# First modulation in quarters beside three open column blocks; a quarter's weights split ahead of it; state space inputs and position tables loaded later

## The chip, the core and the metric

One NeuronCore of a Trainium2 chip runs the whole program. Its engines have a queue of instructions each: PE (matrix products; PEld is its weight load), DVE (vector), ACT (scalar), POOL, and SP, which here only issues DMAs. An instruction that waits holds up everything behind it in its own queue. The metric is the device time of one execution, in microseconds (us).

## The reference, cut to what matters

Two transformer blocks of width 2048 run over 256 tokens, all in f32. The front of the first one computes

```
sh1, sc1, g1, sh2, sc2, g2 = split(silu(c) @ w_ada + b_ada)   # c: one vector of 2048; w_ada: 2048 x 12288
h = rms_norm(x, norm_mix_g) * (1 + sc1) + sh1                 # 256 x 2048
u, q, k, v, ga, gb = split(h @ w_in)                          # w_in: 2048 x 8192; u, q, k, v: 1024 columns each
y = gelu(scan over tokens of a state space model of u)        # 64 groups of 16 channels, 64 complex states each
y_ssm = y * sigmoid(y @ w_glu + b_glu)                        # w_glu: 1024 x 1024
y_att = attention(q, k, v, rel_bias)                          # 8 heads
x = x + g1 * ((sigmoid(ga) * (y_ssm @ w_proj_ssm) + sigmoid(gb) * (y_att @ w_proj_attn)) @ w_out)
```

and then a feed forward part. The second block follows it, and ends in a sparse expert layer that gathers rows of two tables by index. Of the six modulation vectors only sc1 and sh1 (16 MB of w_ada each) are needed before h.

## The kernel before, in words

**Products.** A product of f32 precision is made of three of reduced precision. `piece` loads 1 MB of weights `w` (512 rows of k, 512 columns, as [128, 4, 512]) on the SP queue; ACT makes the high part `wh`, DVE the low part `wl` = w - wh. The activations are split likewise (`h1h`, `h1l` for the first block). For each of the four k-chunks and four column tiles of a piece PE runs three matmuls of 256 columns (the tokens): wh with h1h, wh with h1l, wl with h1h, 48 in all. `gemm` runs four pieces for 512 output columns of a product with k = 2048; two PSUM banks `ga` hold a block's sums. The pools of tiles have 4 buffers for `w` (tag W, shared by the modulation tiles `aw`), 2 for `wh` (H), 2 for `wl` (L), and 14 larger buffers of 1 MB (`unit`).

**The front.** `ada_pe` makes a modulation vector: 16 tiles `aw` of 128 rows by 2048 columns (1 MB each) come in, each goes through PE in four matmuls with f32 operands into `adap` (four column ranges of 512 on four groups of partitions, the same value in each row of a group), ACT copies `adap` to `adae`, four transposes bring it to columns (`adat`), and DVE adds the bias and, for sc1, 1 and the norm's gain, into `mod`. sc1 and sh1 run one after the other (lines 843 and 857). Beside them, paced by `bg`, run the input transposes (`x_in`), the parameters, tables (`ssm_table`, `tab`) and block operands (`ssm_blocks`, `bd` and `cd`, from `ssrc`) of the state space branch, and the position bias (`moba_bias`, `moba_flip`). When sc1 is there, `mod_scale` makes x * rstd * sc1 of a chunk (128 features) in place in `xT`; when sh1 is there, `mod_shift` makes `h1h` (ACT) and `h1l` (DVE) of each chunk:

```
    for i, _ in enumerate(ada_pe(1, 0, None, crep, pacc_, True)):
        if i < NC:
            mod_scale(xp, rstd, mods[(1, 1)], i, xp[i // 2][:, i % 2, :])
        bg(2.3, 0)
```

**What sets the order.** While `pinned[0]` is set, PE, DVE and ACT keep the written order of the instructions issued so far; a scheduler places those issued later, and may move them up between the pinned ones. SP's DMAs stand in one queue in the scheduler's order; each waits for the buffer it fills. After the front, `bg` is called between the matmuls of every piece and issues background work (state space rounds `ssm`, attention, later modulation vectors) by credits: `dve` us of vector work and `rate` modulation tiles a piece.

**After the front.** The blocks of u, q, k and v follow, then ga and gb. `ssm` makes, for four pairs of chunks, `bu` on PE, rotations with the tables on DVE, a scan, and `yp` on PE, which DVE adds into `uT`. Its gelu is split into `zhh` and `zhl`, the operand of the product with w_glu (line 986).

Of the kernel before, what the change touches and what calls it, by code (L numbers as in the profile page):

```python
# [31 lines left out]
def _consts():  # L32
    """Tables that depend on the shapes alone."""
# [40 lines left out]
# Pacing: vector engine time (us) of background work and modulation tiles for each piece of weights.  # L74
# [5 lines left out]
def tile_kernel(ctx: ExitStack, tc: tile.TileContext, I, out):  # L80
# [3 lines left out]
    class Pinned:  # L84
        """An engine whose instructions keep their traced order while `pinned` is set."""
# [52 lines left out]
    # ---------------------------------------------------------------- constants  # L138
# [33 lines left out]
    # ---------------------------------------------------------------- background work  # L172
    # Generators that yield the vector engine time (us) of what they have just issued.
# [39 lines left out]
    # ---------------------------------------------------------------- modulation vectors  # L213
# [31 lines left out]
    def ada(blk, j, g=None):  # L245
        """One modulation vector, its products on the vector engine."""
# [17 lines left out]
    def ada_pe(blk, j, g, crep, pool=pmisc, deep=False):  # L264
        """One modulation vector, its products on the tensor engine."""
# [11 lines left out]

    packs = [
# [24 lines left out]
    # state space parameters, the first modulation vector, the relative position table  # L303
    for t in range(2):
        SY.dma_start(xtok[t], I["x"][0, t * P:(t + 1) * P, :])
# [6 lines left out]
    g_sc1 = ada_pe(1, 1, "norm_mix_g", crep, pacc_, True)  # L312
    src = unit([P, 4, 512], "ssrc")

    def load_src():
        for k, n in enumerate(("ssm_b_re", "ssm_b_im")):
            SY.dma_start(src[:, k, :].rearrange("p (t q) -> p t q", t=32),
                        I[n][0].rearrange("(t g) n q -> (g n) t q", g=2))
        for k, n in enumerate(("ssm_c_re", "ssm_c_im")):
            SY.dma_start(src[:, 2 + k, :].rearrange("p (c n) -> p c n", c=8),  # L320
                        I[n][0].rearrange("(c g) q n -> (g q) c n", c=8))
# [10 lines left out]
    # ---------------------------------------------------------------- norm pieces  # L332
    def rsqrt_of(ps, scale, w, r1=None):
        """(scale ps (r1^2) + eps) ** -0.5 of w columns."""
# [16 lines left out]
    def spread(cols, dst):  # L351
        """Columns of one value a token to rows over the tokens, the same on all partitions."""
# [10 lines left out]
    class Rms:  # L363
        """Mean square over the features of feature-major pairs, a value a token."""
# [26 lines left out]
    def residual(xs, gcol, c, b, quick=False):  # L391
        """x chunks c, c+1 += gate * product."""
# [11 lines left out]
    class HL:  # L404
# [18 lines left out]
        def put2(self, c, src):  # L423
            """Chunks c and c+1 of the operand from an f32 pair."""
# [23 lines left out]
    # ---------------------------------------------------------------- matrix products  # L448
# [75 lines left out]
    # ------------------------------------------------ state space branch  # L524
    def exp_acc(x, shape, alloc):
        """(2^k, q) with exp(x) = 2^k (1 + q), by range reduction and a polynomial."""
# [18 lines left out]
    def ssm_prep():  # L545
# [66 lines left out]
        yield from ssm_table(0)  # L612
        for pp in range(2):
            bc = unit([P, 2, 2, 512], "bct")
            for k in range(2):
                cp2 = 2 * pp + k
                bct[cp2] = [bc[:, k, i, :].rearrange("p (r c m) -> p r c m", r=2, c=2) for i in range(2)]
                yield from ssm_blocks(cp2, src)
        for cp2 in range(1, 3):
            yield from ssm_table(cp2)  # L620

    def ssm_table(cp2):
        """cos and sin of 0..127 times each state's angle, for one pair of chunks (8 state tiles)."""
# [29 lines left out]
    def ssm_blocks(cp2, src):  # L653
        """Block diagonal operands of one pair of chunks."""
# [122 lines left out]
    bias = unit([P, 8, L], "bias")  # L777
# [29 lines left out]
    def x_in():  # L807
# [17 lines left out]
        yield 0.1  # L825

    g_x = start(x_in())
    g_ssm = start(ssm_prep())
    g_col = None
    for i, _ in enumerate(g_sc1):  # L830
        if i == 3:
# [873 lines left out]
```

## Time and profile before

| what | value |
|---|---|
| time, median of 3 runs | 3382.89 us (3382.7 to 3384.3) |
| the profiled execution's span, first to last instruction | 3379.9 us |
| granted TensorE clock, mean over it (1.0 is full speed) | 0.937 |
| busy, of the span: PE, DVE, ACT, POOL | 88%, 68%, 30%, 24% |
| chain that ended last: PE, DMA, issue, DVE, POOL | 62%, 23%, 6%, 4%, 4% |
| DMA traffic | 1068 MB, mean 316 GB/s |

The profiled execution's own time is not listed; its span lies 3.0 us under the median of the runs, and that is taken as what stands around the span. The page's busy shares are means over a front that is fed by transfers, a long middle in which PE is nearly always busy, and an end that gathers expert rows.

### The profile page before, as it was taken

What the parts mean: (1) busy time and instruction counts of PE and PEld (TensorE: products, weight loads), DVE (VectorE), ACT (ScalarE), POOL (GpSimd) and SP (SyncE); (2) the same over time, 40 slices, a digit from 0 to 9 for tenths busy, and PEclk for the clock granted to TensorE, in tenths of its full rate; (3) what the DMA queues carried; (4) which work ended last, traced back from release to release, by engine and by line L of the source; (5) the groups of instructions that cost most, each with busy time, mean ns of one, the idle gap of its engine ahead of it and who ended that gap; (6) DMA issues with size and microseconds to landing.
All of it is one profiled execution on the core that took longest, in us unless ns stands there. A gap on an engine that the chain in (4) does not pass through costs nothing.

```text
span 3379.9 us, 44134 instructions
## 1 busy us (share of the span) xinstructions
PE 2968.7 (88%) x18020; PEld 2299.5 (68%) x18020; DVE 2300.7 (68%) x3359; ACT 1024.1 (30%) x1360; POOL 794.3 (24%) x540
## 2 busy tenths in 40 slices
PE   6899999999999999999999999677876777667777
PEld 2687889999999999999999999333333333223233
DVE  7687779876778778865777668655655566664635
ACT  2323433444444444444347553111111101101100
POOL 1000000000000000000000003666665666665654
PEclk8899999999999999999999999898898889888888
DMA  9866667876899999864783447999999999999998
GB/s 368 301 220 214 202 234 248 305 266 217 295 328 337 320 322 325 324 238 166 259 276 102 138 150 291 418 421 422 421 421 422 422 421 422 421 421 409 422 374 355
DMA packets 278288, 1068.18 MB, mean 316 GB/s; under 512 B 27364, under 2 KB 31879, under 8 KB 187461
## 3 DMA queue, kind: packets, MB, share of 16 engines
q1 hardware_dynamic: 200258, 524.35, 44.3%
q0 software_dynamic: 74752, 538.26, 38.6%
q10 hardware_dynamic: 3076, 2.76, 0.3%
q8 instruction: 141, 2.31, 0.3%
q14 instruction: 61, 0.50, 0.0%
HBM read 1063.19 MB, written 2.11 MB: 315 GB/s over the span
## 4 chain that ended last, share of the span: by engine, by line
PE 62%; DMA 23%; issue 6%; DVE 4%; POOL 4%; ACT 1%; SPq 0%; POOLq 0%; DVEq 0%; ACTq 0%
PE ga L94 47%; DMA dn<-in_peer_down_dram,eid 12%; DMA up<-in_peer_up_dram,eid 9%; PE pe L94 6%; POOL dn L1599 2%; PE gb L94 2%; DMA aw<-in_w_ada_dram 2%; POOL up L1599 2%; PE adap L94 1%; DVE dn L94 1%; PE bu L94 1%; PE rms L94 1%; PE yp L94 1%; PE o L94 1%; PE cmp L94 0%
## 5 line engine op out<-in xcount | busy, mean ns | idle before, releaser
L94 PE MATMUL pe<-up,cdg 128*128 128x512 f32 x1936 | 914.4, 633 | 333.3 <-DMA up<-in_peer_up_dram,eid 202.3
L94 PEld LDWEIGHTS pe<-up,cdg 128*128 128x128 f32 x1936 | 387.7, 204 | 851.7 <-issue 636.7
L1599 POOL DMA_INDIRECT dn<-in_peer_down_dram,eid x256 | 397.7, 1554 | 2252.7 <-DVE rest L94 2003.0
L94 DVE TENSOR_TENSOR wl<-w,wh 128x2048 fp32r<-128x2048 f32 (+1 forms) x300 | 680.5, 2269 | 325.4 <-ACT wh L94 268.5
L94 ACT ACTIVATE wh<-w 128x2048 fp32r<-128x2048 f32 (+1 forms) x300 | 569.2, 1897 | 887.0 <-PE ga L94 715.4
L94 DVE SCALAR_TENSOR_TENSOR dn<-dn,htok 128x2048 f32<-128x2048 f32 x256 | 583.1, 2289 | 325.3 <-DMA dn<-in_peer_down_dram,eid 325.2
L1599 POOL DMA_INDIRECT up<-in_peer_up_dram,eid x256 | 383.6, 1499 | 276.1 <-PE pe L94 108.3
L94 DVE SCALAR_TENSOR_TENSOR acc<-aw,cT,acc 128x2048 f32<-128x2048 f32 x105 | 246.5, 2348 | 16.2 <-DMA aw<-in_ada_w_dram 10.2
L94 PE MATMUL ga<-h2h,wh 128*128 128x256 f32 x1024 | 250.1, 285 | 3.7 <-ACT h2h L94 3.7
L94 PE MATMUL ga<-h2l,wh 128*128 128x256 f32 x1024 | 249.6, 284 | 0.2 <-DVE h2l L94 0.2
L94 PE MATMUL ga<-ah,wh 128*128 128x256 f32 x1024 | 249.3, 283 | 0.0
L94 PE MATMUL ga<-al,wh 128*128 128x256 f32 x1024 | 249.0, 283 | 0.0
L94 ACT ACTIVATE cdg<-ca,cf 128x128 f32<-128x128 f32 x242 | 85.0, 394 | 488.9 <-PE pe L94 464.9
L94 PE MATMUL ga<-h1h,wh 128*128 128x256 f32 x896 | 224.0, 289 | 0.0
L94 PE MATMUL ga<-h1l,wh 128*128 128x256 f32 x896 | 220.4, 284 | 0.0
L94 PEld LDWEIGHTS ga<-h2h,wh 128*128 128x128 f32 x1024 | 197.3, 193 | 5.7 <-ACT h2h L94 4.0
L94 PEld LDWEIGHTS ga<-h2l,wh 128*128 128x128 f32 x1024 | 197.2, 193 | 0.5 <-DVE h2l L94 0.5
L94 PEld LDWEIGHTS ga<-ah,wh 128*128 128x128 f32 x1024 | 196.5, 192 | 0.8 <-ACT wh L94 0.8
L94 PEld LDWEIGHTS ga<-al,wh 128*128 128x128 f32 x1024 | 196.5, 192 | 0.0
L94 PEld LDWEIGHTS ga<-h1h,wh 128*128 128x128 f32 x896 | 172.7, 193 | 19.5 <-issue 15.3
L94 PEld LDWEIGHTS ga<-h1l,wh 128*128 128x128 f32 x896 | 172.9, 193 | 0.9 <-issue 0.8
L94 PE MATMUL ga<-h3h,wh 128*128 128x256 f32 x528 | 133.5, 291 | 1.1 <-ACT h3h L94 1.1
(443 smaller groups left out, 4581.4 us busy)
## 6 DMA issues: line engine op xcount, KB each, us to landing
w<-in_w_ff_dram SPq DMA_DIRECT2D x128, 1024.0 KB, 5.8
w<-in_w_in_dram SPq DMA_DIRECT2D x100, 1024.0 KB, 5.3
aw<-in_w_ada_dram SPq DMA_DIRECT2D x96, 1024.0 KB, 6.9
aw<-in_ada_w_dram SPq DMA_DIRECT2D x96, 1024.0 KB, 5.9
w<-in_w_out_dram SPq DMA_DIRECT2D x32, 1024.0 KB, 5.1
w<-in_peer_wq_dram SPq DMA_DIRECT2D x16, 1024.0 KB, 5.2
w<-in_w_proj_attn_dram SPq DMA_DIRECT2D x8, 1024.0 KB, 5.1
w<-in_w_proj_ssm_dram SPq DMA_DIRECT2D x8, 1024.0 KB, 6.2
```

The costliest lines, as they stand in the source:

```text
L94: r = f(*a, **k)
L1599: G.indirect_dma_start(out=rows_, out_offset=None, in_=table, in_offset=bass.IndirectOffsetOnAxis(ap=idx, axis=0))
```

## The change

`ada_quarter` replaces `ada_pe` for sc1 and sh1: a vector is made in four quarters of 512 columns, each of four tiles `aw` of 512 rows by 512 columns ([128, 4, 512], 1 MB, in pieces of 2 KB a row where they had 8 KB); two of three such tiles take a `unit` buffer, the third a W buffer. A quarter of `mod` gives four chunks of h. With them `first_part` runs one piece (four k-chunks) of three column blocks, u's two and q's first, whose sums stay open in six PSUM banks over all four quarters. The next quarter's tiles are issued between the matmuls of the first two blocks, and the weights of its first two pieces are loaded and split (`first_split`) before that quarter's chunks. x is loaded after two tiles; state space tables 0 and 1 are made beside the front; the loads of `ssrc`, the block operands with table 2, and the position table `moba_bias` are started after the front's code, `moba_flip` after the fourth block, and `ssm` after 16 pieces where it was 8.

```diff
+    def ada_quarter(blk, j, gi, dest, g):
+
+        ps = pmisc([P, 512], "adap")
+        sl = slice(4 * gi, 4 * gi + 4)
+        for k0 in range(0, NC, 4):
+            at[0] += 1
+            wt = wp.tile([P, 4, 512], F32, name=nm("aw"), tag="W") if at[0] % 3 == 0 else unit([P, 4, 512], "aw")
+            SY.dma_start(wt, adaw[blk][k0 * P:(k0 + 4) * P, j * D + 512 * gi:j * D + 512 * gi + 512]
+                         .rearrange("(c p) n -> p c n", p=P))
+            for q in range(4):
+                T.matmul(ps[32 * q:32 * q + 32, :], crep[:, k0 + q, :], wt[:, q, :],
+                         start=(k0 == 0), stop=(k0 == NC - 4), skip_group_check=True)
+            yield 0.0
+        ev = scr([P, 512], "adae")
+        S.copy(ev, ps)
+        pt = pmisc([P, 4, P], "adat")
+        for b in range(4):
+            T.transpose(pt[:, b, :], ev[:, 128 * b:128 * b + 128], ident)
+        V.tensor_reduce(dest[:, sl], pt.rearrange("p b (q r) -> p b q r", q=4)[:, :, :, 0], axis=AX.X, op=OP.add)
+        V.tensor_add(dest[:, sl], dest[:, sl], adab[blk][:, j * 16 + 4 * gi:j * 16 + 4 * gi + 4])
+        if g is not None:
+            V.scalar_tensor_tensor(dest[:, sl], dest[:, sl], 1.0, col[g][:, sl], op0=OP.add, op1=OP.mult)
+        yield 0.4
+
+    at = [0]
...
-    # state space parameters, the first modulation vector, the relative position table
-    for t in range(2):
-        SY.dma_start(xtok[t], I["x"][0, t * P:(t + 1) * P, :])
+    mods[(1, 1)], mods[(1, 0)] = (const([P, 16], "mod") for _ in range(2))
+    def first_mods(gi):
+        yield from ada_quarter(1, 1, gi, mods[(1, 1)], "norm_mix_g")
+        yield from ada_quarter(1, 0, gi, mods[(1, 0)], None)
+    def load_x():
+        for t in range(2):
+            SY.dma_start(xtok[t], I["x"][0, t * P:(t + 1) * P, :])
     ws = unit([P, 16, P], "ws")
     are, aim = ws[:32, 0, :], ws[:32, 1, :]
     S.dma_start(are, I["ssm_a_re"][0].rearrange("(t g) n -> t (g n)", g=2))
     S.dma_start(aim, I["ssm_a_im"][0].rearrange("(t g) n -> t (g n)", g=2))
     ld = tiny([32, 2], "ld")
     S.dma_start(ld, I["ssm_log_dt"][0].rearrange("(t g) -> t g", g=2))
-    g_sc1 = ada_pe(1, 1, "norm_mix_g", crep, pacc_, True)
-    src = unit([P, 4, 512], "ssrc")
+    src = []
     def load_src():
+        src.append(unit([P, 4, 512], "ssrc"))
...
-        yield from ssm_table(0)
+        for cp2 in range(2):
+            yield from ssm_table(cp2)
+
+    def ssm_operands():
         for pp in range(2):
             bc = unit([P, 2, 2, 512], "bct")
             for k in range(2):
                 cp2 = 2 * pp + k
                 bct[cp2] = [bc[:, k, i, :].rearrange("p (r c m) -> p r c m", r=2, c=2) for i in range(2)]
-                yield from ssm_blocks(cp2, src)
-        for cp2 in range(1, 3):
-            yield from ssm_table(cp2)
+                yield from ssm_blocks(cp2, src[0])
+        yield from ssm_table(2)
...
+        revs.append(unit([P, 8, L], "bias"))
...
-    g_x = start(x_in())
-    g_ssm = start(ssm_prep())
-    g_col = None
-    for i, _ in enumerate(g_sc1):
-        if i == 3:
-            load_src()
-        if i == 9:
-            g_col = start(columns())
-        if i == 6:
-            start(moba_bias())
-        if i == NC - 4:
-            drain(g_x, g_col)
-        bg(2.5, 0)
+    g_x = None
+    h = HL(16, "h1")
+    w_in = I["w_in"][0]
+
+    nfirst = 3
+    fb_ = [[(pacc_ if 2 * n + i < 3 else pmisc)([P, 2, L], "ga") for i in range(2)] for n in range(nfirst)]
+
+    def first_split(gi, n):
+        return piece(w_in, 4 * gi, 4, 512 * n, 512)
+
+    def first_part(gi, n, wp_, hook):
+        whi, wlo = wp_
+        for low in (False, True):
+            for i, b in enumerate(fb_[n]):
+                for kk in range(4):
+                    c = 4 * gi + kk
+                    for jj in range(2):
+                        sl = slice((2 * i + jj) * P, (2 * i + jj + 1) * P)
+                        if low:
+                            T.matmul(b[:, jj, :], wlo[:, kk, sl], h.hi(c), start=False, stop=(c == NC - 1),
+                                     skip_group_check=True)
+                        else:
+                            T.matmul(b[:, jj, :], whi[:, kk, sl], h.hi(c), start=(c == 0 and jj == 0), stop=False,
+                                     skip_group_check=True)
+                            T.matmul(b[:, jj, :], whi[:, kk, sl], h.lo(c), start=False, stop=False,
+                                     skip_group_check=True)
+                hook()
+
+    def advance(g, n=1, dve=1.0):
+        for _ in range(n):
+            next(g, None)
+        bg(dve, 0)
+
+    g = first_mods(0)
+    for k in range(10):
+        if k == 4:
+            drain(g_col)
+        if k == 2:
+            load_x()
+            g_x = start(x_in(), first=True)
+            g_col = start(columns(), first=True)
+        advance(g)
+    drain(g_x)
     rstd = r0[0]
-    start(moba_flip())
-    h = HL(16, "h1")
-    for i, _ in enumerate(ada_pe(1, 0, None, crep, pacc_, True)):
-        if i < NC:
-            mod_scale(xp, rstd, mods[(1, 1)], i, xp[i // 2][:, i % 2, :])
-        bg(2.3, 0)
-    pre = []
-    for c in range(NC):
-        mod_shift(xp[c // 2][:, c % 2, :], mods[(1, 0)], c, h)
-        if c in (3, 7):
-            pre.append(piece(I["w_in"][0], c - 3, 4, 0, 512))
+    g_tab = start(ssm_prep())
+
+    ahead_ = [first_split(0, n) for n in range(2)]
+    for gi in range(4):
+        for c in range(4 * gi, 4 * gi + 4):
+            mod_scale(xp, rstd, mods[(1, 1)], c, xp[c // 2][:, c % 2, :])
+            mod_shift(xp[c // 2][:, c % 2, :], mods[(1, 0)], c, h)
+        g = first_mods(gi + 1) if gi < 3 else iter(())
+        first_part(gi, 0, ahead_[0], lambda: advance(g))
+        last = first_split(gi, 2)
+        first_part(gi, 1, ahead_[1], lambda: advance(g))
+        for _ in g:
+            pass
+        if gi < 3:
+            ahead_ = [first_split(gi + 1, 0)]
+        first_part(gi, 2, last, lambda: bg(1.0, 0))
+        if gi < 3:
+            ahead_.append(first_split(gi + 1, 1))
+    load_src()
+    g_blk = start(ssm_operands(), first=True)
+    start(moba_bias())
     pinned[0] = False
...
+    qT = unit([P, 8, L], "qT")
+    kT = unit([P, 8, L], "kT")
+    for n in range(nfirst):
+        ev = store_pairs([uT], 4 * n) if n < 2 else store_pairs([qT], 0, scale=SCALE)
+        for i in range(2):
+            ev(i, fb_[n][i])
+    gemm(w_in, NC, 1536, [("A", 512, store_pairs([qT], 4, scale=SCALE))], h, rate=TUNE["r1"], dve=TUNE["d1"])
+    drain(g_tab, g_blk)
+    start(moba_flip())
     g_ssm = start(ssm())
```

**SP, the end of the front.** Before, with what each DMA waits for: the last tiles of sh1, the first pieces of w_in, and tiles of a later vector.

```order
L270 DMA aw_951<-in_w_ada_dram 128x2048 [waits PE_49]
L270 DMA aw_972<-in_w_ada_dram 128x2048 [waits DMAHW2_49,PE_49]
L270 DMA aw_958<-in_w_ada_dram 128x2048 [waits DMAHW4_49,DMAHW3_49,PE_49]
L270 DMA aw_965<-in_w_ada_dram 128x2048 [waits DMAHW5_49,PE_49]
L451 DMA w_995<-in_w_in_dram 128x4x512 [waits PE_49]
L451 DMA w_1009<-in_w_in_dram 128x4x512 [waits DMAHW6_49,PE_49]
L270 DMA aw_1124<-in_w_ada_dram 128x2048 [waits DMAHW7_49,DMAHW1_49,PE_49]
L451 DMA w_1138<-in_w_in_dram 128x4x512 [waits DMAHW2_49,DMAHW0_49,PE_49]
L451 DMA w_1192<-in_w_in_dram 128x4x512 [waits DMAHW7_49,PE_49]
```

In the change the same place, the last quarter (its eight tiles `aw`, w_1045, w_1164 and w_1262, and after it w_1316 for its third block):

```order
L484 DMA w_1045<-in_w_in_dram 128x4x512 [waits DMAHW0_49,DVE_49]
L285 DMA aw_1227<-in_w_ada_dram 128x4x512 [waits DMAHW7_49,DMAHW3_49,DVE_49]
L484 DMA w_1262<-in_w_in_dram 128x4x512 [waits DMAHW4_49,DMAHW0_49,DVE_49]
L285 DMA aw_1080<-in_w_ada_dram 128x4x512
L285 DMA aw_1116<-in_w_ada_dram 128x4x512
L285 DMA aw_1241<-in_w_ada_dram 128x4x512 [waits DMAHW1_49]
L285 DMA aw_1247<-in_w_ada_dram 128x4x512 [waits DMAHW2_49]
L350 DMA ssrc_1484<-in_ssm_b_re_dram 128x32x16 [waits DMAHW3_49]
L353 DMA ssrc_1484<-in_ssm_c_im_dram 128x8x64 [waits DMAHW6_49]
L484 DMA w_1316<-in_w_in_dram 128x4x512 [waits DMAHW7_49,PE_49]
L484 DMA w_1382<-in_w_in_dram 128x4x512 [waits DMAHW0_49,DVE_49]
```

w_1262, the second weights of the last quarter, waits for DVE with six tiles of that quarter behind it (1080 to 1247), then the four loads of `ssrc`, and then w_1316.

**DVE, the last chunks of h1.** Before: sc1's last chunks, sh1's mod, and the chunks of `h1l` with the first two `wl`.

```order
L94 SCALAR_TENSOR_TENSOR xT_140<-xT_140,mod_141,rstd_403 128x256 x8
L94 TENSOR_TENSOR mod_708<-adat_981,colT_103 128x16
L94 SCALAR_TENSOR_TENSOR h1l_706<-xT_139,mod_708,h1h_704 128x256 x4
L94 TENSOR_TENSOR wl_998<-w_995,wh_997 128x2048
L94 SCALAR_TENSOR_TENSOR h1l_706<-xT_139,mod_708,h1h_704 128x256 x4
L94 TENSOR_TENSOR wl_1012<-w_1009,wh_1011 128x2048
L94 SCALAR_TENSOR_TENSOR h1l_707<-xT_140,mod_708,h1h_705 128x256 x8
L94 TENSOR_TENSOR wl_1141<-w_1138,wh_1140 128x2048
```

In the change, the last quarter's chunks (`xT_138`, `h1l_142`); `rr` is the position table's product, `ba`, `bb`, `bd` and `cd` are operands of the state space branch:

```order
L94 TENSOR_TENSOR wl_1265<-w_1262,wh_1264 128x2048
L94 COPY rrs_1539<-rr_1537 8x512
L94 TENSOR_TENSOR wl_1319<-w_1316,wh_1318 128x2048
L94 SCALAR_TENSOR_TENSOR xT_138<-xT_138,mod_128,rstd_272 128x256
L94 TENSOR_TENSOR ba_1564<-ssrc_1484,prm_135 128x128
L94 TENSOR_SCALAR cd_1606<-ssrc_1484,ca_81 128x2x64 x4
L94 TENSOR_TENSOR bd_1562<-ba_1564,bb_1565 64x8x16 x2
L94 SCALAR_TENSOR_TENSOR h1l_142<-xT_138,mod_129,h1h_140 128x256
L94 SCALAR_TENSOR_TENSOR xT_138<-xT_138,mod_128,rstd_272 128x256
L94 SCALAR_TENSOR_TENSOR h1l_142<-xT_138,mod_129,h1h_140 128x256
L94 SCALAR_TENSOR_TENSOR h1l_142<-xT_138,mod_129,h1h_140 128x256
L94 TENSOR_TENSOR wl_1385<-w_1382,wh_1384 128x2048
```

The four chunks stand one by one, behind `rrs` and wl_1319, and the three remaining pairs' operands stand between them (some of their rows are left out here).

**ACT, the operand of w_glu.** Before: `uT` is the gelu, `zhh` the high part, `wh` those of the pieces around.

```order
L94 ACTIVATE zhh_6109<-uT_1031 128x512 x3
L94 ACTIVATE wh_5994<-w_5992 128x2048
L94 ACTIVATE wh_6051<-w_6049 128x2048
L94 ACTIVATE uT_1031<-uT_1031 128x512
L94 ACTIVATE zhh_6109<-uT_1031 128x512
L94 ACTIVATE wh_6125<-w_6123 128x2048
L94 ACTIVATE wh_6182<-w_6180 128x2048
```

In the change:

```order
L94 ACTIVATE zhh_6150<-uT_1489 128x512 x3
L94 ACTIVATE wh_5981<-w_5979 128x2048
L94 ACTIVATE wh_6038<-w_6036 128x2048
L94 ACTIVATE wh_6166<-w_6164 128x2048
L94 ACTIVATE wh_6223<-w_6221 128x2048
L94 ACTIVATE wh_6294<-w_6292 128x2048
L94 ACTIVATE uT_1489<-uT_1489 128x512
L94 ACTIVATE zhh_6150<-uT_1489 128x512
```

The last pair's gelu and `zhh` stood behind two `wh` and now stand behind five and two `sga`, of which wh_6166 and those after it belong to w_glu itself.

## Rows read from the trace of the kernel before

**Rows 1.** Stages (windows): us, busy PE PEld DVE ACT POOL, clock, DMA, GB/s

```profile
0.00:114.09 114.09, 72.06 (x361) 21.06 (x361) 86.58 (x383) 22.68 (x37) 12.95 (x28) 0.79 0.98 373
...
500.00:640.00 140.00, 140.00 (x1107) 131.95 (x1107) 124.57 (x160) 49.14 (x36) 0.00 (x0) 1.00 0.75 263
```

**Rows 2.** Chain of waits: start, us, engine or DMA, what

```profile
2.61 10.55 DMA aw<-in_w_ada_dram
...
114.09 21.05 PE ga L94 x160
```

**Rows 3.** Timeline of PE, front and first pieces: start, us, instruction

```profile
35.44 1.94 PE L94 MATMUL adap<-aw,crep 128*32 128x512 f32 x8
...
65.07 1.06 PE L94 MATMUL adap<-aw,crep 128*32 128x512 f32 x8
...
108.56 0.66 PE L94 MATMUL adat<-ca,adae 128*128 128x128 f32 x4 [0.76 <-ACT adae L94]
...
114.40 0.42 PE L94 MATMUL ga<-h1l,wh 128*128 128x256 f32 x1
...
121.54 0.28 PE L94 MATMUL ga<-h1h,wh 128*128 128x256 f32 x1
...
127.30 0.28 PE L94 MATMUL ga<-h1h,wh 128*128 128x256 f32 x1
```

**Rows 4.** DVE, 0 to 660 us, groups by form: busy, mean ns, idle before

```profile
L94 DVE TENSOR_TENSOR wl<-w,wh 128x2048 fp32r<-128x2048 f32 x77 | 176.2, 2289 | 80.3 <-ACT wh L94 45.2 <-PE ga L94 17.8 <-issue 12.6
...
L94 DVE SCALAR_TENSOR_TENSOR xT<-xT,mod,rstd 128x256 f32<-128x256 f32 x16 | 7.0, 480 | 0.0
...
L94 DVE SCALAR_TENSOR_TENSOR h1l<-xT,mod,h1h 128x256 fp32r<-128x256 f32 x16 | 6.6, 481 | 0.6 <-ACT h1h L94 0.6
```

**Rows 5.** ACT, 0 to 130 us, groups by form

```profile
L94 ACT ACTIVATE wh<-w 128x2048 fp32r<-128x2048 f32 x4 | 7.6, 1904 | 4.1 <-PE ga L94 4.1
...
L94 ACT ACTIVATE h1h<-xT,mod 128x256 fp32r<-128x256 f32 x16 | 6.7, 495 | 1.0 <-DVE mod L94 1.0
...
L94 ACT COPY adae<-adap 128x512 f32<-128x512 f32 x2 | 1.2, 589 | 22.9 <-PE adap L94 22.9
```

**Rows 6.** Timeline of DVE, a table and a pair's operands

```profile
44.32 0.22 DVE L94 TENSOR_TENSOR ta<-tab,el 128x64 f32<-128x64 f32 x1
...
50.86 0.69 DVE L94 TENSOR_TENSOR ta<-tab,el 128x512 f32<-128x512 f32 x1
...
55.50 0.48 DVE L94 MEMSET bd<- 128x512 f32 x1
...
57.53 0.59 DVE L94 TENSOR_TENSOR bd<-ba,bb 64x128 f32<-64x128 f32 x2
...
60.22 0.87 DVE L94 TENSOR_SCALAR cd<-ssrc,ca 128x128 f32<-128x128 f32 x4
```

**Rows 7.** Timeline of SP's queue: issues, and the time each held it

```profile
19.24 15.94 SPq L317 DMA_DIRECT2D ssrc<-in_ssm_b_im_dram  x1
...
38.97 48.82 SPq L270 DMA_DIRECT2D aw<-in_w_ada_dram  x23
```

**Rows 8.** Windows: ssrc's transfers, then pieces of w_in, then tiles of 8 KB rows

```profile
32.00:42.00 10.00, 8.16 (x28) 3.01 (x32) 8.02 (x40) 0.00 (x0) 0.51 (x1) 0.52 1.01 175
118.00:120.00 2.00, 2.00 (x19) 2.00 (x19) 2.00 (x4) 1.75 (x5) 0.00 (x0) 1.00 1.09 442
132.00:134.00 2.00, 2.00 (x19) 2.00 (x18) 0.69 (x1) 1.25 (x1) 0.00 (x0) 1.00 0.98 364
```

**Rows 9.** DMA issues: what, count, KB each, median us from issue to landing

```profile
w<-in_w_in_dram SPq DMA_DIRECT2D x100, 1024.0 KB, 5.3
```

**Rows 10.** Timeline of DVE at w_glu's operand

```profile
582.48 0.68 DVE L94 TENSOR_TENSOR wr<-bu,tab 128x512 f32<-128x512 f32 x1
...
629.84 0.68 DVE L94 TENSOR_TENSOR zhl<-uT,zhh 128x512 fp32r<-128x512 f32 x1
```

**Rows 11.** Tile zhh: ns of one, least, median, most; first to last

```profile
L94 PE MATMUL ga<-zhh,wh x64: 283/283/283, 638.9 to 659.8; 128*128 128x256 f32 x64
```

More of the change, by code (lines that the diff above doesn't have):

```diff
@@ L311, in tile_kernel @@
     S.dma_start(ld, I["ssm_log_dt"][0].rearrange("(t g) -> t g", g=2))
-    g_sc1 = ada_pe(1, 1, "norm_mix_g", crep, pacc_, True)
-    src = unit([P, 4, 512], "ssrc")
+    src = []
     def load_src():
+        src.append(unit([P, 4, 512], "ssrc"))
         for k, n in enumerate(("ssm_b_re", "ssm_b_im")):
-            SY.dma_start(src[:, k, :].rearrange("p (t q) -> p t q", t=32),
+            SY.dma_start(src[0][:, k, :].rearrange("p (t q) -> p t q", t=32),
                         I[n][0].rearrange("(t g) n q -> (g n) t q", g=2))
         for k, n in enumerate(("ssm_c_re", "ssm_c_im")):
-            SY.dma_start(src[:, 2 + k, :].rearrange("p (c n) -> p c n", c=8),
+            SY.dma_start(src[0][:, 2 + k, :].rearrange("p (c n) -> p c n", c=8),
                         I[n][0].rearrange("(c g) q n -> (g q) c n", c=8))
@@ L776, in tile_kernel @@
     rdr = dr.tile([8, 512], F32, name="rdr")
-    bias = unit([P, 8, L], "bias")
     revs = []
@@ L798, in moba_flip @@
                      rev[:, 2 * k:2 * k + 2, :].rearrange("p h t -> p (h t)"), start=True, stop=True)
-            S.copy(bias[:, 2 * k:2 * k + 2, :], ps)
+            S.copy(revs[1][:, 2 * k:2 * k + 2, :], ps)
             yield 0.6
@@ L863, in need @@
             cred[0] -= step(stream, False)
-    w_in = I["w_in"][0]
     for j, g_ in ((2, None), (4, "norm_mlp_g"), (3, None), (5, None)):
@@ L875, in tile_kernel @@
     uT = unit([P, 8, L], "uT")
-    for nb in range(2):
-        gemm(w_in, NC, nb * 512, [("A", 512, store_pairs([uT], 4 * nb))], h, rate=TUNE["r1"], dve=TUNE["d1"], pre=pre if nb == 0 else ())
-    drain(g_ssm)
+    qT = unit([P, 8, L], "qT")
[7 more added lines that the diff above has]
+    start(moba_flip())
     g_ssm = start(ssm())
@@ L929, in moba @@
             pts = yield from attn_probs([(qT[:, hd + j, :], kT[:, hd + j, :]) for j in range(2)],
-                                        [bias[:, hd + j, :] for j in range(2)])
+                                        [revs[1][:, hd + j, :] for j in range(2)])
             o = pmisc([P, 2, L], "o")
@@ L936, in moba @@
             yield 0.7
-    qT = unit([P, 8, L], "qT")
-    kT = unit([P, 8, L], "kT")
-    for nb in range(2):
-        gemm(w_in, NC, 1024 + nb * 512, [("A", 512, store_pairs([qT], 4 * nb, scale=SCALE))], h, rate=TUNE["r1"], dve=TUNE["d1"])
     for nb in range(2):
```

## The prediction

> **What bounds the kernel now.** I read the stages first. Up to 114.09 us PE is busy 72.06 of 114.09 us at a granted clock of 0.79 while the DMA engines are at 0.98; from 500 to 640 us PE is busy all of the time at 1.00 and the DMA engines at 0.75 [rows 1]. So the front waits for transfers and the middle for PE. The chain of waits says the same: a tile of modulation weights lands at 13.16 us (2.61 + 10.55), and from 114.09 us on PE's `ga` runs with no wait of its own [rows 2]. The gain on offer is PE time in the front: PE could multiply by w_in there if a part of h were known early. Since the middle runs at PE's pace, whatever PE has fallen behind or got ahead when the front's work is done is carried to the end, unless a later wait takes it up.
>
> **Unit prices.** A piece at full clock is 48 matmuls, 121.54 to 127.30: 5.76 us [rows 3]. A tile of `adap` is 1.06 us of PE at full clock and 1.94 at half [rows 3]. wh takes 1.90, h1h 0.50, adae 0.59 [rows 5]; wl 2.29 (starts 2.2 apart, an estimate from its overlap), xT and h1l 0.48 each [rows 4]. A table costs DVE seven doublings of six products each, from 0.2 us (first step) to 0.69 (last); the last two together are 2.8 + 4.3 us, and the steps of 2, 4, 8 and 16 some 6 us, by their rows' growth [rows 6]. The operands of one pair are a memset 0.48, four small products and two bd pairs, some 2.6, and four cd 0.87: about 3.5 to 4 us [rows 6].
>
> Transfers: windows without other traffic moved 442 GB/s (pieces of 2 KB a row) and 364 (among tiles of 8 KB), so a MB takes 2.4 to 2.9 us; I take 2.6 [rows 8]. A lone MB takes 5.3 us from issue to landing [rows 9].
>
> **The change, part by part.** The same 32 MB of modulation weights are loaded, and 12 pieces of w_in (three blocks by four quarters) are multiplied between them.
>
> First matmul of a block. By 13.2 us three MB have landed [rows 2]. The first quarter's last tile is the thirteenth MB in SP's order (x and two pieces stand ahead of it): 13.2 + 10 x 2.6 = 39. Behind it: two tiles through PE at half clock 3.9, adae 0.6, the transposes 1.1, the sum 0.4, then, in written order, the split of the two pieces (1.5 of wh uncovered, two wl 4.4) and a first chunk (1.0): 52 us, where before it was 114.
>
> PE's own work from there to the end of the twelfth piece: 12 x 5.76 = 69.1, 24 tiles x 1.06 = 25.4, six transposes at 0.66 [rows 3] = 4.0, and the columns, `rr` and a few operand transposes 3.5: 102. Without a stall the twelfth piece would end at 154.
>
> The stalls, in the order of the engines' rows:
> a) Each of quarters 1 to 3 starts with wl of its second piece, which needs the `wl` buffer that the third block of the quarter before frees at its end. The four chunks stand behind it on DVE, and each goes xT, h1h, h1l through two engines (0.48 + 0.50 + 0.48, 1.55 with hand-overs) where PE needs 0.96 for a chunk in a column pair. PE waits for wl's rest and first chunk and then paces with the chunks: 4.3 us each, 13 in all (9 if wl starts at once, 16 if the hand-overs are as long as the 1.0 idle of ACT in [rows 5]).
> b) SP: w_457, aw_542, w_699, aw_770 and w_818 stand ahead of aw_574, the last of quarter 1's eight tiles, and wait for the splits, for PE's `adap` and for DVE. When they are let go, aw_574 has one lone transfer and several MB ahead to wait for (5.3 to 3 x 2.6), and the third block stands behind it in PE's order: 8 us (4 to 14).
> c) The same at the next two boundaries, above all w_1262 (W buffer freed by wl_1048, which itself waits for the third block's `wl` buffer) with six tiles of quarter 3 behind it, as the rows of SP show: 5 + 6 = 11 (4 to 20).
> d) The last quarter's chunks on DVE: w_1316 stands behind the four loads of ssrc, of which one held SP 15.94 us [rows 7] in a stretch that moved 175 GB/s for 10 us [rows 8]; then `rrs`, four cd, a memset, wl_1319 and three pairs' operands stand ahead of or between the four chunks, some 14 us in which PE has nothing else to do: 14 (9 if half of it falls into the third block, 25 if ssrc's transfers come in on top).
> e) adae and the transposes of quarters 1 to 3, where PE comes to them before the copy: 2 (2 to 3).
> f) After each wait PE runs at the lower level for a while: the first piece began with 0.42 us a matmul at 114.40, and had 0.28 by 121.54 [rows 3]. Five such starts at about 1 us: 5 (0 to 8).
> Sum 53: the twelfth piece ends at 207 (28 and 182 at the low ends, 86 and 240 at the high ones).
>
> Before, at the same work. 114.1 + 69.1 = 183.2, less what the change has not done by then and must do later (three pairs' transposes 4.65, the position table's flip 3.6, one more tile 1.0, from PE's rows there): 174. So the change is 33 us behind (8 to 66).
>
> Beyond the front. The table steps and operands that DVE no longer does in its 114 us run beside pieces, where DVE is busy 124.57 of 140 [rows 1]. State space rounds start eight pieces later, and the later blocks leave them as many pieces less before w_glu. Before, PE reached w_glu's first product at 638.9 [rows 11] with its last operand ready at 629.84 + 0.68 [rows 10]: 8 us of slack. In the change the last pair's rotations, scan, gelu and split stand, on ACT, behind wh_6166, wh_6223 and wh_6294 of w_glu's own pieces, and on DVE its chain is about 21 us against 11.5 us of PE between its `bu` and its use (half a round of the rows that begin at 582.48 [rows 10], and 3 us for uT, zhh and zhl). I take 13 us (0 if slack remains, 22 if the whole chain is bare). Moved loads cost nothing by themselves: w_in's stream leaves a quarter of the DMA free [rows 1]. The expert part at the end has the same order in both.
>
> Sum: 3379.9 + 33 + 13 = 3426 of span, and 3.0 for what lies around it: 3429. Low ends: + 8 + 0, 3391. High ends: + 66 + 22, 3471.
>
> [...] A piece of 2 KB rows and a tile of 8 KB rows moved alike within the spread of [rows 8] (442 and 364 GB/s, the smaller rows being the faster), so I priced the new shape as the old. [...] Against the change speaks the clock. At 114.40 a matmul took 0.42, later 0.28, after a stretch in which PE waited for tiles [rows 3]. [...]
>
> **The rivals.**
> Overlap holds. If the waits in SP's queue (b, c) are let go before the transfers ahead have run dry, the blocks hide the tiles as drawn: then b, c and f fall away and PE, a little behind, has the chunks ready when it comes to them, which halves a and d or covers them. The twelfth piece ends between 156 and 174, the lead is 0 to 18, and w_glu's slack takes the later state space work: 3375 (3365 to 3383). For it: before, SP's tiles came out 2.1 us apart over 23 issues (48.82 us) [rows 7], a queue that never ran dry. Against it: five waits on engines ahead of aw_574, and chunks that stand behind a buffer which the block before frees. It decides if aw_574 and w_1262 are issued before PE ends the block ahead of them. This is the not slower side.
> State space work hidden. The front as worked out, but the last pair is done in w_glu's slack (8 us before, and a later PE gives DVE more): 3379.9 + 33 + 3.0 = 3416. For it: PE's lag gives DVE the same time back. Against: ACT's order.
> Tiles slower. If tiles of 2 KB rows among pieces come at 2.9 us or more, as the 364 GB/s window would allow, the 32 + 12 MB set the quarters: 0.3 x 44 = 13, some more at the boundaries: 17 over the forecast, 3446. Against: the 442 GB/s window is of that shape.
>
> **How the numbers follow.** Forecast 0.52 (own range 3391 to 3462), overlap holds 0.17, state space hidden 0.19, tiles slower 0.12. 0.2% is about 7 us, which is what a measurement of this kernel can tell from no change. Faster by more: 0.13, from the overlap's case; within it: 0.06, from that case's upper end (0.04) and the forecast's lowest stalls (0.02); slower 0.81. The range 3380 to 3460 leaves out most of the overlap's case below and the highest sums above.
>
> **What would show it.** The first `ga` near 52 us; `ga` of the twelfth piece ending near 207; PE idle before aw_574's `adap` with DMA as its releaser, at each quarter's first `ga` with DVE's h1l as releaser, and some 14 us before the last quarter's; a DMA share well under 0.98 in the front; and PE idle 13 us before zhh's matmuls, released by ACT or DVE. It is wrong if the twelfth piece ends before 174, or if the front's lag does not reach the end.

## The result and the profile after

The changed kernel takes 3430.1 us (median of four runs, 3428.0 to 3431.6) against 3382.8 on the same chip: 1.41% slower, ratio 1.0141 with an interval of 1.0129 to 1.0153. The forecast was 3429. The profiled execution's span is 3427.1 us where it was 3379.9, 47.2 more.

Where the 47 us arise is read from marks that both kernels pass in the same order:

| mark, us | before | after | later by |
|---|---|---|---|
| first `ga` | 114.0 | 52.8 | -61.2 |
| first product of w_glu (`zhh`, wh) | 638.9 | 670.4 | 31.5 |
| last product of w_glu (`zhh`, wl) | 661.8 | 711.4 | 49.6 |
| first product of w_ff1 (`h2h`) | 820.1 | 866.6 | 46.5 |
| last product on `h4h`, ahead of the expert part | 2112.6 | 2163.1 | 50.5 |
| span | 3379.9 | 3427.1 | 47.2 |

So the loss is made in two places: from the first `ga` to the end of the front, and inside w_glu. Between the two, from 212.6 to 670, PE has no wait in either kernel. Behind them 3.1 us are given back up to the first `h2h` (PE waits 1.1 us for it where it waited 3.7), 4.0 more are lost up to `h4h`, and 3.3 are given back in the expert part; the cause of the last was not looked for. First the front, by quarters. The windows (columns as in [rows 1]) run from a quarter's first `ga` to the next one's; [rows 1] had 1.00 once the pieces ran.

```profile
52.81:102.66 49.85, 35.76 (x222) 24.47 (x222) 31.73 (x132) 10.40 (x12) 0.00 (x0) 0.77 0.97 348
102.66:141.66 39.00, 32.47 (x216) 22.29 (x216) 25.09 (x90) 8.85 (x9) 0.00 (x0) 0.85 0.52 162
141.66:182.71 41.05, 35.06 (x226) 23.34 (x226) 23.14 (x57) 8.85 (x9) 0.51 (x1) 0.87 0.98 307
182.71:212.60 29.89, 23.33 (x145) 21.48 (x146) 15.83 (x45) 9.13 (x10) 0.94 (x1) 0.71 0.41 125
```

PE is idle 33.2 of 159.8 us here, and its granted clock is between 0.71 and 0.87. Three pieces, eight tiles and two transposes' groups are 27 us of PE at full clock; the last quarter's three pieces are 17. The list of PE's waits in the same stretch (what waited, for whom, us in total, times, longest):

```profile
PE ga L94 <- ACT h1h L94: 20.6, 4, 6.6
PE adap L94 <- DMA aw<-in_w_ada_dram: 9.6, 2, 8.0
PE ga L94 <- DVE h1l L94: 6.6, 4, 2.2
PE adat L94 <- ACT adae L94: 2.6, 4, 0.7
```

Of the 20.6, 6.6 stand ahead of the first `ga`. The timeline of PE has them in place:

```profile
86.45 1.93 PE L94 MATMUL adap<-aw,crep 128*32 128x512 f32 x8 [7.98 <-DMA aw<-in_w_ada_dram]
...
102.66 0.58 PE L94 MATMUL ga<-h1h,wh 128*128 128x256 f32 x1 [4.97 <-ACT h1h L94]
...
141.66 0.58 PE L94 MATMUL ga<-h1h,wh 128*128 128x256 f32 x1 [5.83 <-ACT h1h L94]
...
149.14 1.93 PE L94 MATMUL adap<-aw,crep 128*32 128x512 f32 x8 [1.57 <-DMA aw<-in_w_ada_dram]
...
182.71 0.54 PE L94 MATMUL ga<-h1h,wh 128*128 128x256 f32 x1 [3.14 <-ACT h1h L94]
185.46 0.58 PE L94 MATMUL ga<-h1l,wh 128*128 128x256 f32 x1 [2.21 <-DVE h1l L94]
```

At 86.45 PE gets quarter 1's last tile 7.98 us late. SP's queue says why (start, us held): a later piece of weights (w_818 of the prediction's list) goes out at 78.11 after its wait, and the tile is the first of the eight DMAs behind it.

```profile
73.15 0.37 SPq L285 DMA_DIRECT2D aw<-in_w_ada_dram  x1
78.11 0.37 SPq L484 DMA_DIRECT2D w<-in_w_in_dram  x1
78.53 23.53 SPq L285 DMA_DIRECT2D aw<-in_w_ada_dram  x8
```

At 102.66 PE waits for a chunk. On DVE the chunks stand behind `wl`, and then go one by one, 1.46 us apart, each with a pause for ACT's h1h:

```profile
99.38 2.28 DVE L94 TENSOR_TENSOR wl<-w,wh 128x2048 fp32r<-128x2048 f32 x1
101.58 0.48 DVE L94 SCALAR_TENSOR_TENSOR xT<-xT,mod,rstd 128x256 f32<-128x256 f32 x1
102.64 0.48 DVE L94 SCALAR_TENSOR_TENSOR h1l<-xT,mod,h1h 128x256 fp32r<-128x256 f32 x1 [0.58 <-ACT h1h L94]
103.04 0.48 DVE L94 SCALAR_TENSOR_TENSOR xT<-xT,mod,rstd 128x256 f32<-128x256 f32 x1
104.09 0.48 DVE L94 SCALAR_TENSOR_TENSOR h1l<-xT,mod,h1h 128x256 fp32r<-128x256 f32 x1 [0.58 <-ACT h1h L94]
```

In [rows 4] the same 16 `xT` and `h1l` waited 0.6 us together, where they ran four or eight in a row.

The rows of SP were read with wrong names for two pieces. In the written order of the code, and in DVE's (wl_1265, wl_1319, the chunks, wl_1385), w_1262 is the last quarter's first piece, w_1316 its second and w_1382 its third. What stands behind w_1262 is as described.

The second place is w_glu. In [rows 11] its products with `zhh` began 20.9 us apart, first to last, with no wait; now 38.9:

```profile
L94 PE MATMUL ga<-zhh,wh x64: 279/283/416, 670.4 to 709.3; 128*128 128x256 f32 x64
```

PE's waits from 600 to 720 us, of which the kernel before had none:

```profile
PE yp L94 <- DVE p L94: 9.1, 1, 9.1
PE ga L94 <- ACT zhh L94: 2.3, 1, 2.3
PE ga L94 <- DVE zhl L94: 0.2, 1, 0.2
```

From the first of these products to the last, before and after (columns as above):

```profile
638.90:661.80 22.90, 22.90 (x193) 22.90 (x192) 16.15 (x10) 12.61 (x14) 0.00 (x0) 1.00 0.86 324
```

```profile
670.40:711.40 41.00, 29.37 (x210) 26.02 (x209) 29.83 (x45) 13.21 (x14) 0.00 (x0) 0.83 0.50 175
```

The stretch is 18.1 us longer: 11.6 of it PE is idle, and 6.5 it is busy longer, with the last pair's 16 `yp` in it and a granted clock of 0.83 where it was 1.00.

### The profile page after: what moved, and what is told of

Read it like the earlier page. It is cut to its first block, busy times and chain, and to the rows that moved or that the text cites. A ratio compares the mean times of both kernels' runs of the same rounds, so it can differ in the third digit from the quotient of the medians.

```text
span 3427.1 us, 44210 instructions
## 1 busy us (share of the span) xinstructions
PE 2987.0 (87%) x18044; PEld 2315.6 (68%) x18044; DVE 2303.6 (67%) x3376; ACT 1026.4 (30%) x1365; POOL 794.4 (23%) x540
## 4 chain that ended last, share of the span: by engine, by line
issue 59%; DMA 20%; PE 10%; DVE 3%; POOL 2%; ACT 0%; POOLq 0%; DVEq 0%; ACTq 0%
DMA dn<-in_peer_down_dram,eid 14%; PE pe L94 10%; DMA up<-in_peer_up_dram,eid 6%; DVE dn L94 1%; POOL dn L1674 1%; POOL up L1674 1%; DVE o L94 0%; DVE rest L94 0%; DVE ix L94 0%; DVE v L94 0%; DVE pick L94 0%; DVE oh L94 0%; DVE vals L94 0%; DVE pf L94 0%; ACT cdg L94 0%
## 5 line engine op out<-in xcount | busy, mean ns | idle before, releaser
L1674 POOL DMA_INDIRECT dn<-in_peer_down_dram,eid x256 | 390.2, 1524 | 2156.7 <-issue 1956.7
L1674 POOL DMA_INDIRECT up<-in_peer_up_dram,eid x256 | 391.3, 1528 | 282.0 <-PE pe L94 113.6
L94 PE MATMUL ga<-h1h,wh 128*128 128x256 f32 x896 | 234.8, 299 | 20.6 <-ACT h1h L94 20.6
L94 PE MATMUL ga<-h1l,wh 128*128 128x256 f32 x896 | 230.2, 293 | 6.6 <-DVE h1l L94 6.6
L94 PEld LDWEIGHTS ga<-h1h,wh 128*128 128x128 f32 x896 | 178.1, 199 | 44.2 <-ACT h1h L94 24.1
L94 PEld LDWEIGHTS ga<-h1l,wh 128*128 128x128 f32 x896 | 178.3, 199 | 11.6 <-DVE h1l L94 10.5
L94 PE MATMUL ga<-ah,wl 128*128 128x256 f32 x1024 | 133.7, 283 | 0.0
```

What stands on the lines that cost most here:

```text
L94: r = f(*a, **k)
L1674: G.indirect_dma_start(out=rows_, out_offset=None, in_=table, in_offset=bass.IndirectOffsetOnAxis(ap=idx, axis=0))
```

## The experiments

Each ran beside the kernel before on its chip; times are medians, a ratio has its interval. The changed kernel had 1.0141 (3430.1, interval 1.0129 to 1.0153). "The third block leaves" is the start of ACT's first copy of q's sums, 212.68 in the change.

**Second split behind the chunks.**

```diff
+        if gi > 0:
+            ahead_.append(first_split(gi, 1))
         g = first_mods(gi + 1) if gi < 3 else iter(())
...
-        if gi < 3:
-            ahead_.append(first_split(gi + 1, 1))
```

> The changed kernel, but each quarter's second weights are split behind that quarter's four chunks of h1 on the vector engine, not ahead of them. Theory (the chunks wait for a wl buffer that the third block frees, and PE's low clock after the wait costs as much again): the waits of 5.0, 5.8 and 3.1 us before a quarter's first ga go, and of the 25 us that PE lost at low clock some 8 to 10: 3430 becomes 3405 to 3413. Rival (transfers set the quarters): PE then waits as long for a tile of the next quarter, and less than 5 us are won: 3425 to 3430. Second rival (the vector engine sets the time until w_glu's operand is ready): the twelfth piece ends earlier, but the wait for yp grows by as much: 3428 to 3432.

3421.4, ratio 1.0118 (1.0103 to 1.0134). The third block leaves at 202.98 where it was 212.68, and w_glu ends 9.5 us earlier: the second rival is out. The gain is 9 us where the theory named 17 to 25. The wait ahead of the last quarter's first `ga` went. The other two went only from 5.0 and 5.8 to 3.2 and 3.6, because table steps of the state space branch now stood directly ahead of the chunks on DVE.

**Operands held back.** The line `pinned[0] = False` moves behind `drain(g_tab, g_blk)`.

> The changed kernel, but the engines keep the written order until the fourth block is done, so that the state space operands stand behind the last quarter's chunks on the vector engine. Theory (term d: operands between the chunks hold PE up): the waits of 2.2, 1.1, 1.6 and 1.7 us inside the last quarter's first block and some 3 us before it go, with some 4 us of low clock: the twelfth piece ends near 202 instead of 212.7, and the whole takes 3418 to 3422. Rival (the same vector work only comes later and the wait for yp before w_glu grows): 3428 to 3434.

3442.1, ratio 1.0181 (1.0168 to 1.0195): slower, which neither expected. The step did what was said (the third block leaves at 200.53, 12 us earlier, and the waits inside the last quarter are 0.3 us in place of 6.6), but with the order kept the fourth block waits for its own weights (`wh`, 2.5 us at a time) and PE is idle 7.4 us between 200 and 240. The fourth block leaves at 248.55 where it was 240.60, so 20 us are lost in it; what the rest of them is was not looked for. So the operands' part of term d is real; this way of removing it costs more.

**State space rounds earlier.** `drain(g_tab, g_blk)`, `moba_flip` and `start(ssm())` go ahead of the fourth block.

> The changed kernel, but the state space rounds start after 12 pieces, ahead of the fourth block, where the change starts them after 16. Theory (the late start makes w_glu wait): the waits of 9.1 us for p and 2.5 us for zhh and zhl shrink or go: 3418 to 3423. Rival (the vector engine is full until w_glu, and the start does not matter): 3428 to 3432.

3418.5, ratio 1.0109 (1.0094 to 1.0125). No wait is left in w_glu: its `zhh` run from 666.3 to 687.2, and w_glu ends at 689.3, 22.1 us before 711.4. Four of these are there already at the third block's end (208.57), where fewer operands stand between the last chunks (3.1 us of waits for h1l there instead of 6.6). By the first `h2h` 21.7 us are won and at the first `yah` 14.1 are left; at the end it is 8.4 in the profiled execution, the slowest of its four, and 11.6 by the medians.

**The late start alone, in the kernel before.**

```diff
-    drain(g_ssm)
-    g_ssm = start(ssm())
...
     for nb in range(2):
         gemm(w_in, NC, 1024 + nb * 512, ...)
+    drain(g_ssm)
+    g_ssm = start(ssm())
```

> The kernel before, with its front as it was; only the state space rounds start after 16 pieces instead of 8. Theory (that start is what makes w_glu wait): the 8 us of slack before zhh's first matmul go and PE waits 5 to 13 us: 3388 to 3396. Rival (the slack and the vector engine's idle time hide it, so w_glu's wait comes from the front's lag or the operands): 3381 to 3385.

3403.4, ratio 1.0070 (1.0056 to 1.0084): 23 us by this part alone, above the theory's 3396. PE waits in w_glu, from 600 to 720 us:

```profile
PE yp L94 <- DVE p L94: 19.0, 2, 11.5
PE ga L94 <- ACT zhh L94: 2.3, 1, 2.3
```

**PE kept busy in the waits.**

```diff
+        if gi > 0:
+            fill = pmisc([P, 4, P], "fill")
+            for b in range(32):
+                T.transpose(fill[:, b % 4, :], ident, ident)
         g = first_mods(gi + 1) if gi < 3 else iter(())
```

> The changed kernel with 32 transposes of a constant (128 x 128, some 0.165 us each, 5.3 us together, into a bank that nobody reads) on PE at the start of quarters 1 to 3, in the place where it waits for the first chunk. Theory (of the 58 us that PE lost between its first ga and the end of the twelfth piece, 33 are waits and 25 are the low clock after them, so a PE that is kept busy in a wait keeps its clock): ga of a quarter's first block starts at 0.28 us instead of 0.41 to 0.58, and 3 us are won a quarter, less what the filler sticks out behind the wait: 3420 to 3426. Rival (the low clock hides beside the pace of the chunks and costs nothing of its own): no gain, or the filler's excess is lost: 3430 to 3436.

3435.8, ratio 1.0162 (1.0148 to 1.0176): in the range of the rival. The filler took 3.65 us and kept the higher clock only for a moment. At quarter 1 that was one matmul:

```profile
96.09 3.65 PE L94 MATMUL fill<-ca 128*128 128x128 f32 x32
101.83 0.38 PE L94 MATMUL ga<-h1h,wh 128*128 128x256 f32 x1 [2.08 <-ACT h1h L94]
102.35 0.58 PE L94 MATMUL ga<-h1l,wh 128*128 128x256 f32 x1
```

The first column pair there takes 5.84 us (101.83 to 107.67) as it did without (102.66 to 108.49, 5.83), but at a granted clock of 0.52 and 0.50, so this pair does not compare two clocks. Quarter 2 does: its first two chunks ran at the higher clock and the next two at the lower, in the same time (its second chunk's matmuls 0.38 and 0.28 us, its third's 0.58 and 0.41):

```profile
140.25:143.16 2.91, 2.01 (x8) 1.20 (x8) 1.76 (x5) 1.01 (x2) 0.00 (x0) 0.98 0.89 265
143.16:146.15 2.99, 2.99 (x8) 2.00 (x8) 2.38 (x7) 0.51 (x1) 0.00 (x0) 0.50 1.05 404
```

So the chunks, 1.46 us apart, set the pair at either clock. In the change itself a column pair whose operands are ready takes 3.41 us at the lower clock, 0.85 a chunk:

```profile
195.18:198.59 3.41, 3.41 (x17) 3.41 (x17) 0.00 (x0) 0.00 (x0) 0.00 (x0) 0.50 0.00 0
```

The third block ends 2.5 us earlier, 0.9 of it from an earlier first `ga`. That the whole takes 6 us more is not clear of noise: the two intervals overlap, and the five executions of this kernel run from 3430.3 to 3438.8. The one profiled, at 3438.5, loses its time far from the change: from the first `h2h` to the first `yah` PE takes 1133.0 us against 1125.3, with 1121.9 busy against 1114.7 for the same matmuls. The end of that stretch, from the last `h3h` to the first `yah`, in the change and then in this run:

```profile
1924.30:1991.90 67.60, 66.53 (x512) 64.41 (x511) 39.19 (x63) 36.85 (x53) 0.00 (x0) 0.95 0.44 147
```

```profile
1928.30:2000.00 71.70, 70.84 (x513) 68.71 (x512) 39.19 (x63) 36.84 (x53) 0.00 (x0) 0.88 0.42 138
```

Nearly the same waits stand in it (1.1 us idle against 0.9), and the clock is lower (0.88 against 0.95). What decides how long it stays low was not tried.

**Together.** The split behind the chunks, the early rounds, four `mod_scale` ahead of four `mod_shift`, and no table steps beside the third block.

```diff
             mod_scale(xp, rstd, mods[(1, 1)], c, xp[c // 2][:, c % 2, :])
+        for c in range(4 * gi, 4 * gi + 4):
             mod_shift(xp[c // 2][:, c % 2, :], mods[(1, 0)], c, h)
...
-        first_part(gi, 2, last, lambda: bg(1.0, 0))
+        first_part(gi, 2, last, lambda: None)
```

> The changed kernel with the second split behind the chunks, the state space rounds started after 12 pieces, all four mod_scale of a quarter ahead of its four mod_shift, and no table steps beside the third block. Theory (each wait has its own cause, so the gains add, and the chunks are ready when the third block ends): 9 us of the split and 12 of the early start, and 3 to 4 us more at each of two boundaries with some low clock behind it: 3395 to 3405. Rival (waits replace each other): no better than the early start alone, 3416 to 3420.

3391.9, ratio 1.0037 (1.0024 to 1.0051), better than the theory's best: 26 us below the early rounds alone. Quarters 1 and 2 start without a wait, the last with 1.5 us, and the third block leaves at 183.30. The wait for the late tile is still there, 7.88 us, and a tile of the next quarter is 3.67 us late.

**And SP in the written order.** `SY` is wrapped as the engines are: `G, SY = nc.gpsimd, Pinned(nc.sync)`.

> As e6_combo, but SP too keeps the written order in the front, so that quarter 1's last tile stands ahead of the next quarter's weights and not behind five waits. Theory (term b: aw_574 late by SP's order): the wait of 8.0 us for it goes with some 3 us of low clock behind: 8 to 11 us below e6_combo. Rival (transfers are the bound there, some tile or piece is late in any order): within 3 us of e6_combo.

3367.2, ratio 0.9962 (0.9949 to 0.9976): below both kernels, 13 us under the one before. The first `ga` comes at 44.9 and the third block leaves at 154.49. That this is the 154 worked out for a front without stalls is chance: the first `ga` is 7 us ahead of the 52 taken there, and 7.6 us are still lost behind it (109.6 for work of 102). From the first `ga` to there:

```profile
44.90:154.50 109.60, 106.36 (x831) 82.65 (x832) 85.76 (x289) 35.60 (x41) 0.00 (x0) 0.98 0.99 345
```

PE is idle 3.2 us at a clock of 0.98, and the DMA engines are at 0.99: both are full at once.

**SP's order alone, on the change.**

> The changed kernel; only SP, too, keeps the written order while the engines are pinned. Theory (term b, and the first tiles queue behind weights that are not yet needed): the first ga comes near 45 us instead of 52.8 and the wait of 8.0 us for quarter 1's last tile goes, so some 14 to 20 us: 3410 to 3416. Rival (the boundaries' waits on chunks take over what the tiles release, and SP's order pays only together with the other edits): 3422 to 3430.

3413.9, ratio 1.0096 (1.0080 to 1.0111): 16 us by the order of one DMA queue. First `ga` at 44.2, no wait for the late tile, third block out at 190.24. That is 22 us of the front; the wait for a chunk at quarter 1 grew from 5.0 to 7.2.

**The same on the kernel before**, as a control.

> Control: the kernel before, with SP keeping the written order as in e8_sp_only. Theory (SP's order matters only where tiles and weights of several quarters mix): 3378 to 3384. Rival (the scheduler's DMA order costs the kernel before as well): 3370 or less.

3381.9, ratio 1.0007 (0.9998 to 1.0016): no change. The edit moves little here: the loads of `ssrc` go out behind four tiles where they stood behind nine. So the control shows that the edit alone changes nothing; that the scheduler's order hurts only where tiles and weights of several quarters mix fits it, and is not shown beyond these two kernels.

**More modulation tiles a piece.** In e7's kernel `"r1"` is 0.75.

> As e7_combo_sp, with the stream of later modulation tiles at 0.75 instead of 0.65 a piece, since the twelve pieces of the front pay nothing into it. Theory (the stream's lag makes PE wait 3.7 us for acc and run at the lower clock after it, near the end of the stage of w_ff1): that wait goes, 4 to 8 us: 3359 to 3363. Rival (the added vector work holds up the split of weights or the state space rounds): 3367 or more.

3374.1, ratio 0.9981 (0.9972 to 0.9990): the rival's range, and no better than e7. The wait for `acc` went, but the wait for p in w_glu came back with 6.0 us.

**More vector work a piece**, in the changed kernel (`"d1"` 4.2) and in e10's.

> The changed kernel with 4.2 us of background vector work a piece instead of 3.6 beside the products of the first half. Theory (w_glu waits because the state space rounds are paced by pieces and get eight fewer, not because the vector engine is full): the 9.1 us wait for p goes, and about 20 us with it, as in e3_early_ssm: 3408 to 3420. Rival (the vector engine is full; more credits only delay the split of weights): 3428 or more.

> As e10_combo_sp_rate, with 4.2 us of background vector work a piece instead of 3.6. Theory (the two paces share the vector engine's credits, and the wait of 6.0 us for p that came back in e10 is a matter of pace): the wait for p goes and the one for acc stays away: 3355 to 3363. Rival (with both paces up the weights' split falls behind): 3367 or more.

3424.3, ratio 1.0124 (1.0108 to 1.0139), and 3369.0, ratio 0.9965 (0.9951 to 0.9978). In e11 the wait for p is gone, w_glu ends 14.1 us earlier and the first `h2h` is 13.7 us earlier; 10 are left at the last `h4h` and 5 at the end. So the wait was one of pace, not of a full vector engine, though the time lies above the range expected, and its interval overlaps that of the change. e12 lost its wait for p too, but lies in its rival's range and ends level with e7: at w_glu's last product it is level (641.4 against 641.1), and ahead of the first `h2h` PE then waits 9.8 us in the norm where it waited 3.7.

## Why the prediction was right

**First `ga`** was put at 52 and came at 52.81. Between 60 and 71 us tiles and pieces, both of 2 KB rows, came at 382 to 389 GB/s in the view of the DMA engines, 2.7 us a MB where 2.6 was taken; the rival of slow tiles, which asked for 2.9 or more, is out.

**The stalls and the clock, a to f**, were put at 53 us and measured 58: PE was idle 33.2 us, and busy 126.6 for work of 102. Of the 24.6 us too many, 15.8 lie in the first column pair of the four quarters (5.83, 5.83, 5.90 and 5.91 us busy, where 16 matmuls take 1.92 at full clock, a third of a piece's 5.76). There the chunks set the pace, so they belong to terms a and d. Counted so:

| term | put | measured |
|---|---|---|
| a, chunks of quarters 1 and 2 (of 1 to 3 as put) | 13 | 18.7 = 4.97 + 5.83 + two paces of 3.9 and 4.0 |
| b, quarter 1's last tile | 8 | 8.0 |
| c, the next boundaries' tiles | 11 | 1.6 |
| d, chunks of the last quarter | 14 | 14.3 = 3.1 + 6.6 + 0.6 + a pace of 4.0 |
| e, copies of `adae` | 2 | 2.6 |
| f, the low clock elsewhere | 5 | 8.8 |
| the pace of the first quarter's chunks | not put | 3.9 |

So the sum is better than its parts. Term c was wrong by 9: w_1262 did hold the six tiles, but PE, late itself, met only one of them late. Term a was too small in its own reading: it took 0.96 us of PE for a chunk in a column pair, which is four matmuls of 0.12, 0.48; and the pace of the first quarter was left out. These errors cancel in part, and that is luck. b was right in place, cause and size, and e8 shows that the order does it; 8.6 us more of e8's gain, at the first `ga`, come from the same order, in a place where the prediction counted the transfers but not that their order could be had better.

The lower clock stood behind the waits of 3.1 to 8.0 us: the first `ga` behind them took 0.54 to 0.58 us and the first `adap` 1.93, at a granted clock of 0.50 to 0.57, where they take 0.28 and 1.06 at full clock [rows 3]. The 5 of term f was an estimate from one such start, and 8.8 was measured. e5 does not settle what the low clock costs beyond the chunks' pace, since the filler did not keep it up for long. The end of the twelfth piece came at 212.6 instead of 207.

**The signs.** ACT's h1h, not DVE's h1l, released each quarter's first `ga`, and 3.1 us, not 14, stood ahead of the last one's; the rest of that term lies between its chunks. The DMA share fell well under 0.98 in two quarters only (0.52 and 0.41), and was 0.97 and 0.98 in the others.

**The lag of the front** was put at 33 us and w_glu's wait at 13. By the marks the lag is 31.5 at w_glu's first product (by the prediction's 174 it is 38.6 at the twelfth piece; 2.7 of the difference are the 16 `yp` that come later, the rest was not traced), and w_glu adds 18.1: its wait was 11.6, near the 13, but 6.5 of longer busy time came with it that the prediction did not count. Undoing the late start (e3) agrees: of the 22.1 us that it takes away at w_glu's last product (689.3 against 711.4), 4.1 are there at the third block's end, which leaves 18.0 for w_glu. e11 gives 14.1, and e4, in the other front, 23.8 (685.6 against 661.8). So w_glu's term was the mis-sized one, 18 where 13 was taken and 22 was the bound, the front's was within 2, and the later stages' 2.4 make the sum of 46 against 47.2 closer than its parts; that too is luck. The rival of hidden state space work is out by the 11.6 us of waits. The reason given for w_glu's wait was half wrong: the last pair's gelu did not stand behind `wh` on ACT; ACT waited 19 us for DVE:

```profile
695.55 0.63 ACT L94 ACTIVATE uT<-uT 128x512 f32<-128x512 f32 x1 [19.19 <-DVE uT L94]
```

The chain of the last pair on DVE was late, as the other half of the reason had it, with a modulation product in it:

```profile
685.23 0.45 DVE L94 TENSOR_TENSOR_SCAN wr<-prm,zin,wr 128x128 f32<-128x128 f32 x1
685.61 2.31 DVE L94 SCALAR_TENSOR_TENSOR acc<-aw,cT,acc 128x2048 f32<-128x2048 f32 x1
687.85 0.67 DVE L94 TENSOR_TENSOR p<-wr,tab 128x512 f32<-128x512 f32 x1
...
694.65 0.87 DVE L94 SCALAR_TENSOR_TENSOR uT<-uT,colT,yp 128x256 f32<-128x256 f32 x2 [3.11 <-PE yp L94]
```

**The rival of the overlap** described the change's idea rightly and its condition too: aw_574 was not issued before PE ended the block ahead of it. e7 meets the condition, and the overlap then holds: the twelfth piece ends at 154.5, and the rival's time of 3365 to 3383 holds e7's 3367.2. It put the lead at 0 to 18 us; 20.7 are there at w_glu's last product (641.1 against 661.8) and 16.8 at the end of the span. Two things in it were not the rival's: the first `ga` comes 7.9 us earlier than in the change, and the state space rounds start after 12 pieces.

**What was left out:** the front's twelve pieces put nothing into the stream of later modulation tiles, so that the last `adap` ran at 619.5 us instead of 511.7 and PE waited 3.7 us for `acc` ahead of w_ff2's products. From the first `h2h` to the first `yah` the change takes 1125.3 us where it was 1120.6; e10 and e12, which give that stream more, have no such wait.

## What to carry to other kernels

When work is interleaved, read the order of each in-order queue, the DMA queue first: here w_818's wait held back the tile behind it, PE got that tile 7.98 us late, and the order of this queue alone was worth 16 us (e8). Work that is paced by pieces loses its credits when pieces are moved into another loop; follow each such stream to its next deadline, since that cost 14 to 24 us here (e11, e3, e4). Remove the waits together: with the chunk's order, the start of the rounds and SP's order put right the same idea went from 47 us slower to 13 faster (e7).

## What was not expected of the hardware

Lifting the clock gave nothing where the chunks on DVE and ACT set the pace: in e5 two chunks took 2.91 us at a granted clock of 0.98 and the next two 2.99 at 0.50. A filler of 3.65 us, with a wait of 2.1 to 2.4 behind it, kept the higher clock for one matmul at one boundary and for two chunks at the next. And two executions with the same matmuls in their middle differ there by 8 us (1125.3 in the change, 1133.0 in e5) through the time that PE stays at its lower clock after nearly the same waits; executions of e5's kernel alone differ by 8.5 us in all, so a gain in the front of less than that may not be seen in a single one.
